# Eight more float32 tiles per layer cut into three float32r products, with their remainders made by transfers and GpSimd

## The chip, the cores and the metric

The kernel runs on one core of one Trainium2 chip. The metric is the device time of one execution in microseconds, taken as the median of several runs. A core has TensorE (PE: matmuls, and PEld: its weight loads), VectorE (DVE), ScalarE (ACT), GpSimd (POOL) and SyncE (SP), each with its own instruction queue that runs strictly in order, and 16 DMA engines that serve the transfers issued from SP's, ACT's and POOL's queues.

## The reference

Two layers over 272 tokens (16 meta tokens and 256 inputs) of width 1024. Each layer is a mixer (a gated causal depthwise convolution beside chunk-causal attention with low-rank projections, joined by two sets of gates), and a product-key expert layer that picks 16 experts per head and token out of 16384.

```python
h = _rmsnorm(x, mix_g); z = h @ w_in
conv_in, c_q, c_kv, k_rope, gate_logits = ...            # columns of z
u = conv_in[..., :512] * sigmoid(conv_in[..., 512:])
u = silu(_layernorm(_causal_depthwise_conv(u, conv_w, conv_b), ...))   # 31 taps
y_conv = u @ w_conv_out
...                                                      # q, k, v from c_q, c_kv, k_rope
y_mla = attention(q, k, v) @ w_mla_out
gates = sigmoid(gate_logits)                             # 2 x 1024 columns
x = x + (gates[..., :1024] * y_conv + gates[..., 1024:] * y_mla) @ w_out

hf = _rmsnorm(x, ffn_g)
q = (hf @ wq).reshape(T, 8, 2, 128)                      # 2048 columns
s = einsum('thpd,hpnd->thpn', q, keys)                   # 128 keys per half
sv, si = top_k(s, 16)                                    # then the top 16 of the 256 sums
a = einsum('ted,td->te', u_table[ids], hf)
x = x + einsum('te,ted->td', gelu(a) * w, v_table[ids])
```

## The kernel before, in words

Activations lie transposed: 128 of the 1024 features per partition block, the 272 tokens along the free dimension (256 in the second layer, where the meta tokens are no longer needed as outputs, `TQ`). Weights come in tiles of 128x1024, two to a transfer (a "pair", 1 MB), in the order in which TensorE uses them. SP issues the pairs; `dma_to` keeps a ring of four pair buffers (`wraw`) ahead, and a load waits until its buffer's last reader is done.

A tile of a projection is eight matmuls of 128x128 weights into one PSUM bank `z`. It is done in one of two ways. `ztile` multiplies in float32; the profile records each such matmul twice. `three` splits weights and activations into a part rounded to float32r ("high") and the remainder ("low") and adds three products, high by high, low by high and high by low, 24 matmuls. `high(i, n)` makes the rounded weight part on ACT, from the tile n places ahead; `low(i)` makes the remainder, in one of three ways: a subtraction on VectorE, the same on GpSimd, or (tiles 21, 23, 25, 27) a second copy on ACT with the sign turned followed by an accumulating transfer from POOL's queue that adds the raw weights. `kinds` says in which old buffers the two parts lie (`wq0`/`wq1`, `seln`/`upad`, `acc`/`sqa`, `kh`, `sq`).

Order of a layer: projections for attention; four pairs of convolution inputs (c = 0 to 3); sixteen gate tiles g0 to g15 (`TPG` names those cut in three); attention output, convolution output and merging tiles; sixteen query tiles (numbers 16 to 31 in `parts`, here query tiles 0 to 15); then the expert stages: 128 tiles of u weights (`A`) and 128 of v weights (`po`). Most token-expert pairs of 160 tokens go through dense matmuls in the expert stages, the other tokens through gathers: POOL fetches one 8 KB row per partition (`uv`), VectorE multiplies and adds it.

Beside the gate tiles, attention runs as a generator `att` stepped by hand twice a tile, and the 31 convolution taps run on VectorE (`conv`, `taps`, a number per tile in `TAPS`). For channel block 0 the first `KD` = 21 taps are products on ACT, added up by accumulating transfers into `part` (`conv2`); VectorE adds the three columns of `part` to `acc` at the end of `conv2`. When all taps are in, `layernorm` begins with the sum `tot` (tile name `zkr`), which a matmul with ones reads.

Beside the query tiles, VectorE picks top-16 values from the scores of the tile before (`scores`, `top16`), and a generator `early` prepares the expert numbers of the first tokens; `spread(0, 0, nc.sync)` sends them by a transfer on SP. Nine pairs of u weights are loaded ahead outside the ring: `EARLY` lists the pairs, `EPLACE` says after which query tile each is issued and into which buffer (own buffers `we`, or `kh`, `sq`, `g0`, `g1`, whose former contents are then done with; `g0` and `g1` hold the normalised input of the query tiles in two parts, `xq`).

Of the kernel before, what the change touches and what calls it, by code (L numbers as in the profile page):

```python
# [7 lines left out]
F32 = mybir.dt.float32  # L8
# [5 lines left out]
OP = mybir.AluOpType  # L14
# [8 lines left out]
KW = 31  # L23
# [2 lines left out]
WS = 16384.0  # L26
TAPS = [6, 6, 7, 8] + [9] * 12
KD = 21
TPG = (10, 11, 12, 13, 14, 15)
SCALE = 96 ** -0.5  # L30
NC_ = 58
GROUPS = ((64, 32), (64, 32))

EARLY = (0, 1, 2, 3, 8, 10, 12, 14, 16)
EPLACE = {1: (4, None), 4: (0, "kh"), 5: (5, None), 7: (6, None), 8: (7, None), 9: (1, "sq"), 11: (8, None), 12: (2, "g0"), 13: (3, "g1")}
JS = 63
MIXQ = {"xg", "uk", "qr", "rq_w", "rq_x", "rq_ym", "tkw0", "tkw1", "tkw2", "tkm", "sk", "scs", "qm",
        "wq0", "wq1", "seln", "upad", "acc", "sqa", "g0", "g1"}
LASTP = 2
RU = ((1.75, 1.45), (1.65, 1.33))  # L40
# [13 lines left out]
def trunk_kernel(ctx: ExitStack, tc: tile.TileContext, a: dict, out: bass.AP, dbg=None, stop=None):  # L54
    nc = tc.nc
# [9 lines left out]
    srcs = []  # L65
# [146 lines left out]
    for l in range(NL):  # L212
# [11 lines left out]
        def two(name):  # L224

            t_ = tw.tile([128, 8 * T], F32, name=name, tag=name)
            return t_[:, 0:2048]

        mixs = ExitStack()
        mixb = ExitStack()  # L230
        mpa = mixs.enter_context(tc.tile_pool(name=f"mixq{l}", bufs=1))
        mpb = mixb.enter_context(tc.tile_pool(name=f"mix{l}", bufs=1))

        class mp:

            @staticmethod
            def tile(shape, dt, name, **kw):
                return (tw if name in ("sq", "kh", "g0", "g1") else mpa if name in MIXQ else mpb).tile(shape, dt, name=name, **kw)
        zs = ExitStack()
        zp = zs.enter_context(tc.tile_pool(name=f"z{l}", bufs=1, space=PSUM))  # L240

# [423 lines left out]
        def conv2():  # L665

            for k in range(0, KD, 3):
                u_ = mp.tile([128, 3, T], F32, name="cp", bufs=2) if k else part
                for x in range(3):
                    S.activation(u_[:, x, t0:], upad[:, 0, k + x + t0:k + x + T], AF.Copy, scale=weight(0, k + x))  # L670
                    yield
                if k:
                    G.dma_start(part[:, :, t0:], u_[:, :, t0:], accum_op=OP.add)
            for _ in range(2):
                yield
            while ck[0] == KD:
                yield
            for x in range(3):
                V.tensor_add(acc[:, 0, t0:], acc[:, 0, t0:], part[:, x, t0:])
            yield  # L680

        parts = {}

        xhs_ = []
        kinds = {"g10": 0, "g11": 1, "g12": "k", "g13": 0, "g14": 1, "g15": "s", 0: "k", 1: 0, 2: 1, 3: "s", 4: "k",
                 19: "k", 20: "a", 21: "q", 22: "w", 23: "s", 24: "q", 25: "a", 26: "s", 27: "w"}

        def high(i, n):

            w_ = peek_w(n)  # L690
            x = kinds[i] if i in kinds else "aws"[(i - 5) % 3]
            if x == "w":
                hi, lo = [mp.tile([128, 1024], F32, name=f"wq{y}") for y in range(2)]
            elif x == "s":
                hi = mp.tile([128, 1024], F32, name="seln")
                lo = mp.tile([128, 1208], F32, name="upad")[:, 0:1024]
            elif x == "a":
                hi = mp.tile([128, 4 * T], F32, name="acc")[:, 0:1024]
                lo = mp.tile([128, 4 * T], F32, name="sqa")[:, 0:1024]
            elif x in (0, 1):  # L700
                if not xhs_:
                    xhs_.append(pp.tile([128, 8 * T], F32, name="xh"))
                hi = mp.tile([128, 1024], F32, name=f"wq{x}")
                lo = xhs_[0][:, 1024 * x:1024 * x + 1024]
            else:
                t_ = mp.tile([128, 8 * T], F32, name="kh" if x == "k" else "sq", tag="kh" if x == "k" else "sq")
                hi, lo = t_[:, 0:1024], t_[:, 1024:2048]
            parts[i] = hi.bitcast(F32R), lo.bitcast(F32R), w_
            S.activation(parts[i][0], w_, AF.Copy)
            if i in (21, 23, 25, 27):  # L710
                S.activation(parts[i][1], w_, AF.Copy, scale=-1.0)

        def low(i):

            hi, lo, w_ = parts[i]
            if i in (21, 23, 25, 27):
                G.dma_start(lo, w_, accum_op=OP.add)
            else:
                (G if i in (20, 22, 24, 26) else V).tensor_tensor(lo, w_, hi.bitcast(F32), op=OP.subtract)

        def three(i, p, xs, wc, cs, first, end, mid=None):

            hi, lo, _ = parts[i]
            for c in cs:
                s_ = slice((wc + c) * 128, (wc + c + 1) * 128)
                mm(p, hi[:, s_], xs[0][:, c, t0:], c == first, False)
                mm(p, lo[:, s_], xs[0][:, c, t0:], False, False)
                mm(p, hi[:, s_], xs[1][:, c, t0:], False, c == end)
                if c == 3 and mid:
                    next(mid, None)  # L730
# [78 lines left out]
        def taps(n, m, cs=(0, 1, 2, 3)):  # L809
            conv(n, cs)  # L810
            for _ in range(m):
                next(cvp, None)
# [4 lines left out]
        for c in range(4):  # L817
# [17 lines left out]
            if c == 2:  # L835
                xnh = big("uk", [8, T], F32R)
                xnl = mp.tile([128, 8, T], F32, name="un").bitcast(F32R)
                for k in range(8):
                    S.activation(xnh[:, k, t0:], xg[:, k, t0:], AF.Copy)
                    V.tensor_tensor(xnl[:, k, t0:], xg[:, k, t0:], xnh[:, k, t0:].bitcast(F32), op=OP.subtract)  # L840
            taps((0, 0, 8, 6)[c], (0, 3, 4, 4)[c], (1, 2, 3)[:max(c, 1)])
            next(att, None)

        gt = [big("g0", [8, T]), big("g1", [8, T])]
        ln = None
# [13 lines left out]
        for i in range(16):  # L859
# [3 lines left out]
                three(f"g{i}", z, (xnh, xnl), 0, range(8), 0, 7, ln if lnk == 2 else None)  # L863
            else:
                z = ztile(t0)
            new = [f"g{i + 2}"] if i + 2 in TPG else []
            ns = [1] if new else []
            for j in {13: (0,), 14: (1,)}.get(i, ()):
                new.append(j)
# [4 lines left out]
            S.activation(gt[i // 8][:, i % 8, t0:], z, AF.Sigmoid if ex else AF.Copy)  # L874
            if not ex:
                todo.append(i)
            if i >= 14:
                high(i - 12, 3)
            if i == 14:
# [100 lines left out]
        residual(7)  # L980
        normal(7)
        mixb.close()
        if stop == f"mix{l}":
            dump(stop, hT)
            for s_ in (asx, zs, mixs, twos, rp):
                s_.close()
            return
# [168 lines left out]
        for i in range(16):  # L1156
# [3 lines left out]
                three(16 + i, z, xq, 0, range(8), 0, 7)  # L1160
            else:
                z = ztile(t0)
            for k in {0: (2, 3), 1: (5,), 2: (4,), 3: (7,), 4: (6,), 5: (9,), 6: (8,), 7: (11,), 8: (10,)}.get(i, ()):
                high(16 + k, k - i - 1)
                low(16 + k)
            if i in EPLACE:
                k, n = early_[l][EPLACE[i][0]], EPLACE[i][1]
                raws[k] = (two(n).rearrange("p (a b) -> p a b", a=2) if n else
                           ep.tile([128, 2, 1024], F32, name=f"we{i}"))
                nc.sync.dma_start(raws[k], srcs[k])  # L1170
            qT_ = mp.tile([128, T], F32, name="qr", bufs=2)
            S.activation(qT_[:, t0:], z, AF.Copy)
            if not last:
# [576 lines left out]
```

## Time and profile before

| | us |
|---|---|
| median of 3 runs (1659.16 to 1660.91) | 1660.8 |
| the profiled execution | 1659.62 |
| its span | 1657.8 |
| TensorE busy | 1642.4 (99%) |
| VectorE busy | 1261.6 (76%) |
| ACT busy | 693.3 (42%) |
| POOL busy | 333.0 (20%) |
| DMA mean | 343 GB/s |

The page divides the span into 40 slices of about 41 us; a digit is the busy share of a slice in tenths. In a timeline a row is: start, duration, engine, line, operation, output and inputs by name, shapes, number of merged instructions, and in brackets the idle time before it and what ended it. A row of the chain of waits is start, duration, engine and what ran. The line L62 is the helper that issues every matmul, so matmuls are told apart by tile names. A windows row gives the stretch, its length, busy time and count of PE, PEld, DVE, ACT and POOL, then TensorE's granted clock, the DMA share and GB/s. TensorE's granted clock is full throughout.

### The profile page before, as it was taken

The page shows a single profiled execution, that of the slowest core. Times are in us where ns is not written, and L with a number is a line of the kernel's source. Part 1 is how long each engine was busy: PE and PEld are TensorE (multiplying, and loading weights), DVE is VectorE, ACT ScalarE, POOL GpSimd, SP SyncE. Part 2 cuts the span into 40 slices and gives each one's busy share as a digit, 9 for nine tenths or more (in the row PEclk, how much of TensorE's full clock was granted, in tenths as well). Part 3 has the DMA queues.
Part 4 walks back from the last instruction along what each step waited for, and adds up shares of the span by engine and source line. Part 5 has one row for each costly group of instructions (what it writes and reads, how often), then busy time and mean ns, then how long its engine had stood idle before and what let it go on. Part 6 is the DMA issues. An engine that isn't in the chain of part 4 may idle for free.

```text
span 1657.8 us, 30712 instructions
## 1 busy us (share of the span) xinstructions
PE 1642.4 (99%) x11827; PEld 1468.5 (89%) x11827; DVE 1261.6 (76%) x3082; ACT 693.3 (42%) x1803; POOL 333.0 (20%) x347
## 2 busy tenths in 40 slices
PE   9999999999999999999999999999999999999999
PEld 7679999999999999999986899999999997566655
DVE  5799899897898544444447998897877886788885
ACT  3565733435554111000024576433445443455554
POOL 0000033221222222222200100432211222233330
PEclk9999999999999999999999999999999999999999
DMA  6444697999999999999962746989999999999994
GB/s 249 113 128 177 242 345 298 424 383 424 416 423 418 424 424 423 424 424 424 417 259 85 176 153 242 340 348 396 362 425 409 409 391 411 420 425 425 424 425 191
DMA packets 86099, 568.52 MB, mean 343 GB/s; under 512 B 10328, under 2 KB 15384, under 8 KB 18744
## 3 DMA queue, kind: packets, MB, share of 16 engines
q1 hardware_dynamic: 50608, 338.51, 50.7%
q0 software_dynamic: 34560, 227.31, 35.0%
q8 instruction: 93, 1.52, 0.4%
q10 hardware_dynamic: 784, 0.74, 0.1%
q14 instruction: 54, 0.44, 0.1%
HBM read 556.18 MB, written 1.05 MB: 336 GB/s over the span
## 4 chain that ended last, share of the span: by engine, by line
PE 87%; DMA 8%; DVE 3%; ACT 1%; issue 1%; POOL 0%; SPq 0%; DVEq 0%; ACTq 0%; POOLq 0%
PE A L62 34%; PE po L62 25%; PE z L62 20%; DMA wraw<-vt 5%; PE aps L62 5%; PE wp L62 2%; DMA X<-vt 2%; DMA sqa<-wraw 1%; DVE acc L661 1%; PE xp L62 0%; PE sc L62 0%; DVE xh L1549 0%; PE wp L1262 0%; DVE tkw L1008 0%; ACT wr L1547 0%
## 5 line engine op out<-in xcount | busy, mean ns | idle before, releaser
L62 PE MATMUL A<-xh,wraw 128*128 128x160 f32 x3520 | 498.0, 300 | 0.0
L62 PEld LDWEIGHTS A<-xh,wraw 128*128 128x128 f32 x3520 | 481.1, 190 | 0.0
L62 PE MATMUL z<-xg,wraw 128*128 128x272 f32 (+2 forms) x832 | 194.1, 392 | 0.0
L1440 DVE SCALAR_TENSOR_TENSOR g<-g,xr 128x1024 f32<-128x1024 f32 x94 | 114.8, 1221 | 90.8 <-DMA g<-uv,iww 90.8
L62 PEld LDWEIGHTS z<-xg,wraw 128*128 128x128 f32 (+1 forms) x832 | 151.8, 189 | 35.0 <-issue 5.8
L1415 POOL DMA_INDIRECT g<-uv,iww x94 | 113.6, 1209 | 306.3 <-DVE va L1425 197.4
L1451 ACT ACTIVATE am<-am 128x1 f32<-128x1 f32 x208 | 40.9, 196 | 312.1 <-DVE g L1440 157.8
L62 PE MATMUL po<-Xh,wraw 128*128 128x160 f32 x1040 | 143.1, 300 | 1.0 <-DMA wraw<-vt 0.9
L62 PEld LDWEIGHTS po<-Xh,wraw 128*128 128x128 f32 x1040 | 141.5, 190 | 2.0 <-DMA wraw<-vt 2.0
L62 PE MATMUL po<-X,wraw 128*128 128x160 f32 x1008 | 138.4, 299 | 1.8 <-DMA wraw<-vt 1.3
L62 PEld LDWEIGHTS po<-X,wraw 128*128 128x128 f32 x1008 | 137.1, 190 | 2.7 <-DMA wraw<-vt 1.0
L1425 DVE SCALAR_TENSOR_TENSOR va<-g,am,va 128x1024 f32<-128x1024 f32 x91 | 116.5, 1281 | 0.3 <-ACT am L1452 0.2
L1340 ACT ACTIVATE ohA<-ohE,wlo 128x128 f16<-128x128 f16 x320 | 105.3, 428 | 5.2 <-DVE ohE L1337 4.4
L1440 DVE SCALAR_TENSOR_TENSOR kh<-kh,xr 128x1024 f32<-128x1024 f32 x48 | 58.6, 1221 | 42.5 <-DMA kh<-uv,iww 42.5
L1440 DVE SCALAR_TENSOR_TENSOR sq<-sq,xr 128x1024 f32<-128x1024 f32 x48 | 58.7, 1222 | 39.4 <-DMA sq<-uv,iww 39.4
L1415 POOL DMA_INDIRECT sq<-uv,iww x48 | 58.0, 1209 | 151.1 <-DVE va L1425 90.6
L1415 POOL DMA_INDIRECT kh<-uv,iww x48 | 59.9, 1248 | 140.4 <-DVE va L1425 92.8
L661 DVE SCALAR_TENSOR_TENSOR acc<-upad,cols,acc 128x272 f32<-128x272 f32 (+1 forms) x198 | 83.0, 485 | 0.2
L1351 ACT ACTIVATE Xh<-wp 128x260 f32<-128x260 f32 (+19 forms) x80 | 24.6, 307 | 131.5 <-DVE Xh L1348 124.8
L1425 DVE SCALAR_TENSOR_TENSOR va<-sq,am,va 128x1024 f32<-128x1024 f32 x48 | 61.5, 1281 | 5.5 <-ACT am L1452 5.5
L1425 DVE SCALAR_TENSOR_TENSOR va<-kh,am,va 128x1024 f32<-128x1024 f32 x48 | 61.5, 1282 | 3.7 <-ACT am L1452 3.7
L1452 ACT ACTIVATE am<-am,iww 128x1 f32<-128x1 f32 x208 | 61.3, 295 | 6.9
(503 smaller groups left out, 3075.0 us busy)
## 6 DMA issues: line engine op xcount, KB each, us to landing
wraw<-u SPq DMA_DIRECT2D x110, 1024.0 KB, 9.2
wraw<-vt SPq DMA_DIRECT2D x109, 1024.0 KB, 12.2
wraw<-w_in SPq DMA_DIRECT2D x27, 1024.0 KB, 4.7
X<-vt SPq DMA_DIRECT2D x17, 1024.0 KB, 11.4
wraw<-wq SPq DMA_DIRECT2D x16, 1024.0 KB, 4.8
we<-u SPq DMA_DIRECT2D x10, 1024.0 KB, 12.1
wraw<-w_out SPq DMA_DIRECT2D x8, 1024.0 KB, 4.6
wraw<-w_mla SPq DMA_DIRECT2D x4, 1024.0 KB, 5.1
```

What stands on the lines that cost most here:

```text
L62: PE.matmul(o, l, r, start=start, stop=stop, skip_group_check=True)
L661: V.scalar_tensor_tensor(acc[:, c, t0:], u_, weight(c, k), acc[:, c, t0:], op0=OP.mult, op1=OP.add)
L1340: S.activation(A_[1][:, t // 2, :, t % 2], E[0][:, t // 2, :, t % 2], AF.Copy, scale=wlo[:, 4 * b + t:4 * b + t + 1])
L1351: S.activation(x_, p[:, :, a:b].rearrange("p t j -> p j t"), AF.Copy, scale=1.0 / WS)
L1415: G.indirect_dma_start(out=g_, out_offset=None, in_=a[f"uv{l}"], in_offset=bass.IndirectOffsetOnAxis(ap=iww[i].bitcast(I32)[:, m // 16, 0, ...
L1425: V.scalar_tensor_tensor(vac[i], r, m_, vac[i], op0=OP.mult, op1=OP.add)
L1440: V.scalar_tensor_tensor(u_, u_, 1.0, xrs[i], op0=OP.mult, op1=OP.mult, accum_out=m_)
L1451: S.activation(m_, m_, AF.Gelu_apprx_tanh)
L1452: S.activation(m_, m_, AF.Copy, scale=iww[i][:, m // 16, 1, m % 16:m % 16 + 1])
```

## The change

Gate tiles 1, 3, 5 and 7 and query tiles 12 to 15 (28 to 31 in `parts`) become three-product tiles. The remainders of the gates and of tiles 30 and 31 are made by the accumulating transfer (now listed in `BYDMA`), those of 28 and 29 by subtraction on GpSimd. Tiles made by transfer run their products in another order: eight high by high, eight high by low activation part, and the eight with the remainder last. Gates 3 and 7 get a new buffer `gp`. In `conv2` the three adds of `part` wait until every tap of every block is in. The early pairs get new places; the ones in `sq`, `g0`, `g1` and one `we` come later, three `we` loads sooner, and since `g0` and `g1` are read until the last query tile, two loads are issued after tile 15. The work tiles of the top-16 (`ONLYQ`) go to a pool opened after the mixer's memory is released.

```diff
-TPG = (10, 11, 12, 13, 14, 15)
+TPG = (1, 3, 5, 7, 10, 11, 12, 13, 14, 15)
+ONLYQ = {"tkw0", "tkw1", "tkw2", "tkm", "scs", "qm"}
-EPLACE = {1: (4, None), 4: (0, "kh"), 5: (5, None), 7: (6, None), 8: (7, None), 9: (1, "sq"), 11: (8, None), 12: (2, "g0"), 13: (3, "g1")}
+EPLACE = {1: (4, None), 2: (5, None), 4: (0, "kh"), 5: (6, None), 6: (7, None), 13: (1, "sq"), 14: (8, None), 15: (2, "g0"), 15.5: (3, "g1")}
+BYDMA = ("g1", "g3", "g5", "g7", 21, 23, 25, 27, 30, 31)
-MIXQ = {"xg", "uk", "qr", "rq_w", "rq_x", "rq_ym", "tkw0", "tkw1", "tkw2", "tkm", "sk", "scs", "qm",
+MIXQ = {"xg", "uk", "qr", "rq_w", "rq_x", "rq_ym", "sk",
...
@@ conv2
-            for _ in range(2):
-                yield
-            while ck[0] == KD:
+            while min(ck.values()) < KW:
                 yield
             for x in range(3):
                 V.tensor_add(acc[:, 0, t0:], acc[:, 0, t0:], part[:, x, t0:])
-            yield
...
-        kinds = {"g10": 0, ..., 27: "w"}
+        kinds = {"g1": "v", "g3": "p", "g5": "v", "g7": "p", "g10": 0, ..., 27: "w", 28: "q", 29: "a", 30: "s", 31: "w"}
@@ high
-            if x == "w":
+            if x == "p":
+                t_ = mp.tile([128, 2048], F32, name="gp")
+                hi, lo = t_[:, 0:1024], t_[:, 1024:2048]
+            elif x in ("w", "v"):
                 hi, lo = [mp.tile([128, 1024], F32, name=f"wq{y}") for y in range(2)]
...
-            if i in (21, 23, 25, 27):
+            if i in BYDMA:
                 S.activation(parts[i][1], w_, AF.Copy, scale=-1.0)
@@ low
-            if i in (21, 23, 25, 27):
+            if i in BYDMA:
                 G.dma_start(lo, w_, accum_op=OP.add)
             else:
-                (G if i in (20, 22, 24, 26) else V).tensor_tensor(lo, w_, hi.bitcast(F32), op=OP.subtract)
+                (G if i in (20, 22, 24, 26, 28, 29) else V).tensor_tensor(lo, w_, hi.bitcast(F32), op=OP.subtract)
@@ three
+            if i in BYDMA:
+                for w_, x, f, e in ((hi, xs[0], first, None), (hi, xs[1], None, None), (lo, xs[0], None, end)):
+                    for c in cs:
+                        mm(p, w_[:, c * 128:(c + 1) * 128], x[:, c, t0:], c == f, c == e)
+                return
@@ convolution inputs, at the end of a pair
+            if c == 2:
+                high("g1", 3)
+                low("g1")
             taps((0, 0, 8, 6)[c], (0, 3, 4, 4)[c], (1, 2, 3)[:max(c, 1)])
             next(att, None)
+            if c == 3:
+                high("g3", 3)
+                low("g3")
@@ gate tiles
-            new = [f"g{i + 2}"] if i + 2 in TPG else []
+            new = [f"g{i + 2}"] if i >= 8 and i + 2 in TPG else []
...
+            if i in (1, 3):
+                high(f"g{i + 4}", 3)
+                low(f"g{i + 4}")
@@ after mixb.close()
+        qo.append(mixs.enter_context(tc.tile_pool(name=f"qo{l}", bufs=1)))
@@ query tiles
-            for k in {0: (2, 3), 1: (5,), ..., 8: (10,)}.get(i, ()):
+            for k in {0: (2, 3), 1: (5,), ..., 8: (10,), 9: (12,), 10: (13,), 11: (14, 15)}.get(i, ()):
                 high(16 + k, k - i - 1)
                 low(16 + k)
-            if i in EPLACE:
-                k, n = early_[l][EPLACE[i][0]], EPLACE[i][1]
...
+            for e in (i, i + 0.5):
+                if e in EPLACE:
+                    k, n = early_[l][EPLACE[e][0]], EPLACE[e][1]
...
```

More of the change, by code (lines that the diff above doesn't have):

```diff
@@ L230, in trunk_kernel @@
         mixb = ExitStack()
+        qo = []
         mpa = mixs.enter_context(tc.tile_pool(name=f"mixq{l}", bufs=1))
@@ L237, in tile @@
             def tile(shape, dt, name, **kw):
-                return (tw if name in ("sq", "kh", "g0", "g1") else mpa if name in MIXQ else mpb).tile(shape, dt, name=name, **kw)
+                return (tw if name in ("sq", "kh", "g0", "g1") else qo[0] if name in ONLYQ else mpa if name in MIXQ else mpb).tile(shape, dt, name=name, **kw)
         zs = ExitStack()
@@ L679, in conv2 @@
                 V.tensor_add(acc[:, 0, t0:], acc[:, 0, t0:], part[:, x, t0:])
-            yield
         parts = {}
         xhs_ = []
-        kinds = {"g10": 0, "g11": 1, "g12": "k", "g13": 0, "g14": 1, "g15": "s", 0: "k", 1: 0, 2: 1, 3: "s", 4: "k",
-                 19: "k", 20: "a", 21: "q", 22: "w", 23: "s", 24: "q", 25: "a", 26: "s", 27: "w"}
+        kinds = {"g1": "v", "g3": "p", "g5": "v", "g7": "p", "g10": 0, "g11": 1, "g12": "k", "g13": 0, "g14": 1, "g15": "s", 0: "k", 1: 0, 2: 1, 3: "s", 4: "k",
+                 19: "k", 20: "a", 21: "q", 22: "w", 23: "s", 24: "q", 25: "a", 26: "s", 27: "w", 28: "q", 29: "a", 30: "s", 31: "w"}
         def high(i, n):
@@ L1162, in trunk_kernel @@
                 z = ztile(t0)
-            for k in {0: (2, 3), 1: (5,), 2: (4,), 3: (7,), 4: (6,), 5: (9,), 6: (8,), 7: (11,), 8: (10,)}.get(i, ()):
+            for k in {0: (2, 3), 1: (5,), 2: (4,), 3: (7,), 4: (6,), 5: (9,), 6: (8,), 7: (11,), 8: (10,), 9: (12,),
+                      10: (13,), 11: (14, 15)}.get(i, ()):
                 high(16 + k, k - i - 1)
                 low(16 + k)
-            if i in EPLACE:
-                k, n = early_[l][EPLACE[i][0]], EPLACE[i][1]
-                raws[k] = (two(n).rearrange("p (a b) -> p a b", a=2) if n else
-                           ep.tile([128, 2, 1024], F32, name=f"we{i}"))
-                nc.sync.dma_start(raws[k], srcs[k])
+            for e in (i, i + 0.5):
+                if e in EPLACE:
+                    k, n = early_[l][EPLACE[e][0]], EPLACE[e][1]
+                    raws[k] = (two(n).rearrange("p (a b) -> p a b", a=2) if n else
+                               ep.tile([128, 2, 1024], F32, name=f"we{i}"))
+                    nc.sync.dma_start(raws[k], srcs[k])
             qT_ = mp.tile([128, T], F32, name="qr", bufs=2)
```

## The prediction

> **What bounds the kernel now.** I read the page first: busy times, slices, chain. Its lines carry the first answer.
>
> ```profile
> span 1657.8 us, 30712 instructions
> PE 1642.4 (99%) x11827; PEld 1468.5 (89%) x11827; DVE 1261.6 (76%) x3082; ACT 693.3 (42%) x1803; POOL 333.0 (20%) x347
> GB/s 249 113 128 177 242 345 298 424 383 424 416 423 418 424 424 423 424 424 424 417 259 85 176 153 242 340 348 396 362 425 409 409 391 411 420 425 425 424 425 191
> PE 87%; DMA 8%; DVE 3%; ACT 1%; issue 1%; POOL 0%; SPq 0%; DVEq 0%; ACTq 0%; POOLq 0%
> ```
>
> TensorE (PE) is busy 99% of the span and holds 87% of the chain, so matmul time removed counts wherever no other engine catches up. The bytes per slice show two regimes in each layer: the mixer and query projection (slices 1 to 6 and 21 to 27 of 40) run at 85 to 350 GB/s, while the expert stages after them sit near 424. The change edits only the first regime, so I next read those stretches, in time order: the chain, then VectorE's (DVE) timeline with its waits, then ACT, POOL and SP.
>
> **The matmul saving.** Rows of the chain: plain tiles (eight float32 products, 16 records) and tiles cut in three products (24 records), 272 columns in layer 1 and 256 in layer 2.
>
> ```profile
> 63.53 7.34 PE z L62 x32
> 171.20 27.13 PE z L62 x216
> 921.52 6.91 PE z L62 x32
> 1005.40 25.53 PE z L62 x216
> ```
>
> A plain tile is 7.34/2 = 3.67 us, a three-product tile 27.13/9 = 3.01: 0.66 saved. In layer 2 it is 6.91/2 - 25.53/9 = 3.46 - 2.84 = 0.62. Each layer converts eight tiles (gates 1, 3, 5, 7; query tiles 12 to 15): 8 x 0.66 + 8 x 0.62 = 10.2 us of TensorE time gone.
>
> **The gate half: does VectorE let it through?** VectorE runs the convolution taps there almost without a break. These are its waits, the end of its convolution sum, and the TensorE product that reads it; layer 1, then layer 2.
>
> ```profile
> 80.34 1.48 DVE L469 TENSOR_TENSOR kh<-kh,aps 96x272 f32<-96x272 f32 x4 [0.58 <-PE aps L62]
> 112.43 1.36 DVE L492 TENSOR_REDUCE mx<-aps 128x1 f32<-128x144 f32 x4 [1.55 <-PE aps L62]
> 132.60 0.92 DVE L747 TENSOR_TENSOR zkr<-zkr,acc 128x272 f32<-128x272 f32 x2
> 133.87 0.73 PE L62 MATMUL aps<-zkr,ones 128*128 128x272 f32 x2
> 938.58 1.36 DVE L492 TENSOR_REDUCE mx<-aps 128x1 f32<-128x144 f32 x4 [0.94 <-PE aps L62]
> 949.57 1.36 DVE L492 TENSOR_REDUCE mx<-aps 128x1 f32<-128x144 f32 x4 [1.98 <-PE aps L62]
> 970.19 0.67 PE L62 MATMUL aps<-zkr,ones 128*128 128x256 f32 x2 [0.67 <-DVE zkr L747]
> ```
>
> Nothing leaves VectorE: the new gate tiles' remainders are made by accumulating transfers, and the three adds of the transferred taps move to the end of the taps, 3 x 0.46 (the zkr row's 0.92/2) on both sides of the move: nothing, as VectorE is busy from one place to the other. What VectorE can gain is its waits on TensorE. Layer 1: 0.58 + 1.55 = 2.13, while TensorE gains 4 x 0.66 = 2.64. The sum was ready at 133.52 and used at 133.87, so the new wait is (133.52 - 2.13) - (133.87 - 2.64) = 0.16 us. Layer 2: waits of 0.94 + 1.98 = 2.92 exceed TensorE's 4 x 0.62 = 2.48, so that half passes whole and the 0.67 wait stays.
>
> Their price on ACT and POOL: each of the four tiles adds two copies on ACT and one transfer on POOL's queue.
>
> ```profile
> 1045.36 1.05 ACT L711 ACTIVATE sqa<-wraw 128x1024 fp32r<-128x1024 f32 x1
> 63.67 2.67 ACT L839 ACTIVATE uk<-xg 128x272 fp32r<-128x272 f32 x8
> 94.77 0.47 ACT L498 ACTIVATE pr<-aps,nb,sc 128x144 f32<-128x144 f32 x1 [3.97 <-DVE nb L493]
> 75.72 3.93 PE L62 MATMUL z<-xg,wraw 128*128 128x272 f32 x16
> DMA to landing us min/median/max: 4.1/4.9/8.3
> ```
>
> Two copies are 2.1 us. For gate 7 they fall into the 3.97 us that ACT waits before the second softmax; cover gone, they would delay it by up to 2.1. Gate 1 is the tight one: ACT is free of the operand copies at 66.3, the pair is done at 68.4, and transfers of this queue at this place (the taps' own, last line) land in 4.1 to 8.3, so by 72.5 to 76.7. Gate 1 begins at 75.72 and reads the remainder only after 16 of its 24 products, 2.0 us later. I take zero; if it took 12.6 us (the longest below) it would cost 3.3 per layer.
>
> **The query half: when do the remainders arrive?** In order: the scattered-index copy that holds ACT, POOL's subtraction and its four scalings, the landing times of today's four such transfers per layer, tile 14's start in both layers, and a stall of today's tile 9.
>
> ```profile
> 230.96 1.91 ACT L1064 ACTIVATE tx<-it 128x2048 f16<-128x2048 f16 x1 [3.71 <-DVE it L1062]
> 224.77 2.39 POOL L719 TENSOR_TENSOR upad<-wraw,seln 128x1024 fp32r<-128x1024 f32 x1 [0.39 <-ACT seln L709]
> 227.12 2.95 POOL L1205 TENSOR_TENSOR xh<-xg,rq_ym 128x272 f32<-128x272 f32 x4
> DMA to landing us min/median/max: 6.2/9.1/12.6
> 246.94 3.83 PE L62 MATMUL z<-xg,wraw 128*128 128x272 f32 x16
> 1060.59 1.91 ACT L1064 ACTIVATE tx<-it 128x2048 f16<-128x2048 f16 x1 [2.99 <-DVE it L1062]
> 1077.17 3.62 PE L62 MATMUL z<-xg,wraw 128*128 128x256 f32 x16
> 1059.56 0.38 PE L62 MATMUL z<-g,sqa 128*128 128x256 f32 x1 [1.67 <-DMA sqa<-wraw]
> ```
>
> Tiles 12 and 13 are subtracted on GpSimd, 14 and 15 by transfer, and all four go through POOL in order, between scalings of 2.95/4 = 0.74. Layer 1: ACT is free at 232.9, tile 12's copy ends 233.9, its subtraction 236.3, a scaling 237.1, tile 13's subtraction 239.5, a scaling 240.2; then tile 14's transfer starts. TensorE reaches tile 14 at 246.94 - 2 x 0.66 = 245.6 and needs the remainder 16 x 0.126 = 2.0 later, 247.6. At the median 9.1 it lands at 249.3: a wait of 1.7. Layer 2: 1062.5, 1063.6, 1065.9, 1066.7, 1069.1, 1069.8; needed at 1077.17 - 1.67 - 2 x 0.62 + 1.9 = 1076.2, landing 1078.9: a wait of 2.7. So 4.4 us are given back; tile 15's transfer, one issue later, is needed 3 us later still and is covered. Ends: at 6.2 nothing, at 12.6 it is 5.2 + 6.2 = 11.4. I take the median because it is the same instruction in the same stage, and a pair of early loads joins the queue right at that time. [...]
>
> The reordering of the products (all those with the high part first) also applies to today's transferred tiles. Tile 9 of layer 2 stalls 1.67 for a remainder it now needs 1.9 later: 1.7 gained (0 if its transfer lands that much later).
>
> **Early pairs, queues, memory.** Pairs 2 and 3 of the expert weights are loaded after tile 15, since their buffers now hold the query operand until then. On SP they stand behind the index spread, which waits for VectorE.
>
> ```profile
> 255.31 0.62 SPq L1150 DMA_DIRECT2D iww<-ew  x1
> 254.72 1.42 PE L62 MATMUL sc<-uk,qr 128*128 128x128 f32 x8
> 257.09 4.61 PE L62 MATMUL A<-xh,kh 128*128 128x160 f32 x32 [0.59 <-ACT idxT L1036]
> 266.76 8.45 PE L62 MATMUL A<-xh,g 128*128 128x160 f32 x61
> 255.00:265.00 10.00, 9.30 (x73) 8.73 (x73) 9.39 (x72) 4.75 (x10) 3.55 (x4) 1.00 0.28 88
> wraw<-w_out SPq DMA_DIRECT2D x8, 1024.0 KB, 4.6
> kh<-uv,iww POOLq DMA_INDIRECT x1, 14.5
> 260.54 1.08 POOL L1415 DMA_INDIRECT X<-uv,iww  x1 [30.46 <-DVE ts L1006]
> ```
>
> They issue at about 255.9. The expert stage will start 2.37 after tile 15 ends, at 254.72 - 4 x 0.66 + 1.7 + 2.37 = 256.2, and reads pair 2 after 266.76 - 257.09 = 9.7, at 265.8: 9.9 us of cover. The window shows DMA at 88 GB/s there, and a quiet megabyte takes 4.6, so I take zero. The worst near row is a gather in the crowd, 14.5: 4.6 per layer. Pair 1 (after tile 12, issue near 241) has 19 us. Behind the two loads on SP wait only the meta-row copies of layer 1, which need VectorE later still.
>
> The top-16 work tiles move to a pool of their own, outside the memory that the first gathers fill; those gathers waited for VectorE's top-16 until 260.54 though the index was sent at 255.31. They may start up to 2.5 us sooner per layer; I take nothing, since the expert weights, not they, are next on TensorE.
>
> **What the expert stages do with an earlier start.** DMA is full there, so an earlier TensorE could just wait for weights.
>
> ```profile
> PE po L62 <- DMA wraw<-vt: 2.2, 6, 0.7
> 836.05 1.28 DVE L1425 SCALAR_TENSOR_TENSOR va<-g,am,va 128x1024 f32<-128x1024 f32 x1
> 842.91 1.85 PE L62 MATMUL xp<-zs,va 128*128 128x16 f32 x16
> ```
>
> Waits for weights are 2.2 us in all, and layer 1's last gather is added 5.6 us before TensorE needs it (842.91 - 837.33). TensorE will be 2.5 + 2.6 - 1.7 = 3.4 early, VectorE and so the gathers at least 2.1: a lag of 1.3, inside that 5.6. I take zero.
>
> **Sum.** -10.2 + 0.16 - 1.7 + 4.4 = -7.3 us. The profiled execution took 1659.62, 1.2 under the median 1660.8 of the runs; 1652.3 in its terms is 1653.5 against the median. No change means within 0.2%, 3.3 us.
>
> **Rivals.** (1) The remainders land in time (6.2): -11.7, 1649.1. For it: by the new places three loads leave the time just before it. Against: by SP's order three megabyte loads (pair 1, a ring pair, pair 16) go out near 241, and the 9.1 median. [...] (2) The transfer-full expert stages give the query half back and only the gates' shift survives, 2.1 + 2.5 = 4.6: 1656.2. For it: 424 GB/s in nearly every slice; against: 2.2 us of waits and 5.6 of cover. Chance 0.17. (3) The remainders land at worst (12.6): -0.3, 1660.5, chance 0.09. (4) Slower: pair 2 is late. Its place is the third pair of each expert stage; the loads share DMA with the first gathers. At 14.5 us it costs 2 x 4.6 = 9.2, giving 1662.7 with the rest as summed; it turns the sign above 9.9 + 3.7 = 13.6 us. Against: DMA is nearly idle when they issue. Chance 0.08.
>
> **Numbers.** My forecast 0.46 (its own range 1651 to 1656), the rivals as given. Faster by over 0.2%: 0.46 + 0.20 + most of 0.17, 0.81; same 0.09 and the remainder, 0.12; slower 0.07. The range runs from rival 1 with gathers a little early, 1647, to between rivals 2 and 3, 1658.
>
> **What would show it.** Gates 1, 3, 5, 7 at 3.0 and 2.84 us; waits at 112 and 949 gone from VectorE; a wait of TensorE on the transfers into upad (tile 14) of 1 to 3 us in each layer, and none on sqa; the third expert pair without a wait; the last gather add of layer 1 still ahead of its sum. I am wrong if TensorE waits on the loads into g0 and g1, on gate 1's remainder, or if waits on wraw<-vt grow by more than 2 us.

## The result, and the profile after

The change made the kernel slower: 1672.8 us (median of 6 runs, 1668.5 to 1675.3) against 1659.2 for the kernel before on the same chip (6 runs, 1657.0 to 1660.9). The ratio is 1.0078, 95% interval 1.0061 to 1.0095. The profiled execution took 1673.24 us, its span is 1671.5, so 13.7 more than the span of before. The prediction was 1653.5, its range 1647 to 1658.

The page, the parts that were shown of before:

```profile
span 1671.5 us, 31046 instructions
PE 1643.3 (98%) x11955; PEld 1474.8 (88%) x11955; DVE 1261.4 (75%) x3082; ACT 717.8 (43%) x1831; POOL 356.9 (21%) x363
PE 79%; DMA 11%; DVE 5%; ACT 2%; issue 1%; POOL 1%; SPq 0%; DVEq 0%; POOLq 0%; ACTq 0%
```

TensorE's busy time did not fall by 10 us, it rose by 0.9, and of the 8 points of share that TensorE lost in the chain of what ended last DMA and VectorE (DVE) took 5. Fewer products and slower products cancel in the busy time: the mean granted clock of this execution is 0.993, of before 1.000, and 0.007 of the span is 11.7 us (an estimate; it counts waits at the lower clock too). The rest of the loss is waits. TensorE's waits (us in all, times, longest), and the rows of the chain that belong to transfers (start, duration, both in us):

```profile
PE z L64 <- DMA wq<-wraw: 7.0, 2, 4.1
PE z L64 <- DMA gp<-wraw: 2.6, 1, 2.6
PE aps L64 <- DVE zkr L755: 2.1, 2, 1.6
```

```profile
69.51 8.83 DMA part<-cp
240.26 13.37 DMA wq<-wraw
913.67 11.48 DMA part<-cp
931.72 10.74 DMA part<-cp
1079.56 13.50 DMA wq<-wraw
```

Two places, each once per layer. `wq<-wraw` at 240 and 1079 is tile 15's remainder: 13.4 and 13.5 us from issue to landing. `part<-cp` is a transfer of taps; their landing times were 4.1/4.9/8.3 before and are now:

```profile
DMA to landing us min/median/max: 4.4/8.1/11.5
```

To put the loss on places, I cut the span at six points of TensorE's timeline: a product of z near 59 us, the product of zkr (end of the gate half), the first expert pair (end of the query half), and in layer 2 its first product, zkr and the first expert pair. Four of these rows in after:

```profile
133.56 0.70 PE L64 MATMUL aps<-zkr,ones 128*128 128x272 f32 x2 [0.50 <-DVE zkr L755]
257.89 6.53 PE L64 MATMUL A<-xh,kh 128*128 128x160 f32 x32 [0.59 <-ACT idxT L1054]
978.46 1.03 PE L64 MATMUL aps<-zkr,ones 128*128 128x256 f32 x2 [1.60 <-DVE zkr L755]
1097.46 6.58 PE L64 MATMUL A<-xh,kh 128*128 128x160 f32 x32 [0.53 <-ACT idxT L1054]
```

Before, the same stages took 74.6, 123.2 and 590.9 us (gates, queries, experts of layer 1), then 122.2, 116.3 and 571.3. The table gives each kernel's difference from these in us, worked out from the start times in its own trace; a minus is time saved. The times are medians of 5 to 12 runs, the ratios are to the runs of the kernel before on the same chip, with their 95% intervals. The stages come from one profiled execution each; single executions of a kernel scatter by 2 to 9 us. Furthest from their medians are those of gates_only (3.7 above), gates_notrans (1.9 below) and queries_warm (2.1 below).

```
kernel            us      ratio [95%]             gates1 query1 expert1 gates2 query2 expert2
after           1672.8  1.0078 [1.0061, 1.0095]    0.0   +1.1   +3.2   +4.2   +2.7   +2.7
gates_only      1666.1  1.0037 [1.0023, 1.0051]   +0.2   -0.1   +0.5   +9.6   -0.6   +0.5
gates_pool      1666.3  1.0038 [1.0025, 1.0051]   +3.0   -0.1   +0.9   +3.3   +0.6   -0.1
gates_notrans   1657.2  0.9986 [0.9977, 0.9995]   -0.8   -0.1   -0.1   -1.1   -2.0    0.0
gates_57        1659.4  0.9988 [0.9977, 0.9999]   -1.3   -0.1   +0.2   +2.1   -0.5   -0.6
queries_only    1667.2  1.0039 [1.0026, 1.0052]   +0.5   +1.3   +1.3   +0.9   +1.8   +1.4
queries_pool    1660.9  1.0004 [0.9995, 1.0013]   +0.5   -1.9   +3.2   +0.9   -1.6   +1.7
queries_notrans 1655.9  0.9976 [0.9967, 0.9986]   +0.5   -2.7   +0.6   +1.0   -3.1   -0.1
queries_quiet   1671.6  1.0069 [1.0055, 1.0083]   +0.5   -2.0   +6.4   +0.9   +0.6   +6.7
queries_warm    1663.1  1.0017 [1.0009, 1.0026]   +0.5   +0.3   +0.4   +0.9   +0.1   -0.5
neither         1661.5  1.0005 [0.9996, 1.0014]   +0.5   -0.1   +1.8   +0.9   -0.5   +0.4
q1214           1654.8  0.9966 [0.9953, 0.9979]    0.0   -2.0   +0.1    0.0   -3.7   +1.1
best            1658.2  0.9987 [0.9978, 0.9996]   -1.3   -1.4   +0.8   +2.2   -1.1   +0.5
```

**The gate half.** GpSimd's queue (POOL), ACT and VectorE in time order; the first row is of before, the same transfer as in the second:

```profile
72.82 0.89 POOL L673 DMA_DIRECT2D part<-cp  x1 [3.83 <-ACT cp L670]
78.87 0.85 POOL L676 DMA_DIRECT2D part<-cp  x1 [8.39 <-DMA part<-cp]
925.70 1.29 POOL L676 DMA_DIRECT2D part<-cp  x1 [10.60 <-DMA part<-cp]
```

```profile
78.42 0.93 ACT L673 ACTIVATE cp<-upad,cols 128x272 f32<-128x272 f32 x2 [6.19 <-DMA part<-cp]
79.26 1.04 ACT L712 ACTIVATE gp<-wraw 128x1024 fp32r<-128x1024 f32 x1
925.24 0.91 ACT L673 ACTIVATE cp<-upad,cols 128x256 f32<-128x256 f32 x2 [8.71 <-DMA part<-cp]
```

```profile
88.26 0.18 DVE L507 RECIPROCAL sm<-sm 128x4 f32<-128x4 f32 x1 [2.34 <-ACT pr L501]
934.74 0.18 DVE L507 RECIPROCAL sm<-sm 128x4 f32<-128x4 f32 x1 [4.97 <-ACT pr L501]
945.05 0.18 DVE L507 RECIPROCAL sm<-sm 128x4 f32<-128x4 f32 x1 [2.49 <-ACT pr L501]
```

The taps' transfers all add into one tile (`part`), so GpSimd issues each only when the last has landed. Gate 1's 512 KB go out just before the first of them; that one lands late, and GpSimd stands 8.4 us (10.6 in layer 2) before it can issue the next, in layer 1 6 us later than before (78.87, before 72.82). The taps' two buffers (`cp`) stay full, and ACT, which works in order, stands 6.2 us (8.7 in layer 2) before its next copy into one. Behind that copy stand gate 3's copies and the softmax, and VectorE waits for the softmax: 2.3 us in layer 1, 7.5 in layer 2. Gate 3's remainder is late by the same chain in layer 2, the 2.6 us on gp.

**The query half.** TensorE at tile 15, and its granted clock (the last three columns of a window are clock, DMA share and GB/s):

```profile
253.67 1.27 PE L64 MATMUL z<-g,wq 128*128 128x272 f32 x8 [2.83 <-DMA wq<-wraw]
1093.10 2.08 PE L64 MATMUL z<-g,wq 128*128 128x256 f32 x8 [4.12 <-DMA wq<-wraw]
```

```profile
250.00:260.00 10.00, 6.58 (x39) 5.53 (x38) 9.16 (x48) 1.65 (x7) 1.27 (x2) 0.75 0.79 279
1090.00:1100.00 10.00, 6.37 (x25) 6.07 (x26) 6.81 (x35) 1.75 (x6) 1.88 (x2) 0.56 0.86 317
```

TensorE stands 2.8 and 4.1 us with the high part's 16 products done. After that its clock is 0.75 and 0.56 of full in the ten microseconds around (in windows of two microseconds it reads 0.50 from 1092 to 1100 us and 1.00 again from 1102), and the first expert pair, the same 32 products as before, takes 6.53 and 6.58 us instead of 4.61: 1.9 us more in each layer, which appear in the table under "expert". No wait on tile 14 (upad) is left, none on sqa, and none on pairs 2 and 3.

### The profile page after: what moved, and what is told of

It is laid out like the page before. It is cut to its first block, busy times and chain, and to the rows that moved or that the text cites. A ratio compares the mean times of both kernels' runs of the same rounds, so it can differ in the third digit from the quotient of the medians.

```text
span 1671.5 us, 31046 instructions
## 1 busy us (share of the span) xinstructions
PE 1643.3 (98%) x11955; PEld 1474.8 (88%) x11955; DVE 1261.4 (75%) x3082; ACT 717.8 (43%) x1831; POOL 356.9 (21%) x363
## 4 chain that ended last, share of the span: by engine, by line
PE 79%; DMA 11%; DVE 5%; ACT 2%; issue 1%; POOL 1%; SPq 0%; DVEq 0%; POOLq 0%; ACTq 0%
PE A L64 34%; PE po L64 26%; PE z L64 12%; DMA wraw<-vt 5%; PE aps L64 3%; DVE acc L664 3%; PE wp L64 2%; DMA part<-cp 2%; DMA wq<-wraw 2%; DMA X<-vt 1%; DMA wraw<-wq 1%; PE xp L64 0%; PE sc L64 0%; DVE mx L495 0%; DMA wraw<-w_in 0%
## 5 line engine op out<-in xcount | busy, mean ns | idle before, releaser
L1435 POOL DMA_INDIRECT g<-uv,iww x94 | 117.4, 1249 | 308.5 <-DVE va L1445 195.6
L64 PE MATMUL z<-xg,wraw 128*128 128x272 f32 (+2 forms) x576 | 134.4, 394 | 0.4 <-DMA wraw<-w_in 0.4
L64 PEld LDWEIGHTS z<-xg,wraw 128*128 128x128 f32 (+1 forms) x576 | 104.3, 188 | 27.4 <-issue 4.9
```

What stands on the lines that cost most here:

```text
L64: PE.matmul(o, l, r, start=start, stop=stop, skip_group_check=True)
L1435: G.indirect_dma_start(out=g_, out_offset=None, in_=a[f"uv{l}"], in_offset=bass.IndirectOffsetOnAxis(ap=iww[i].bitcast(I32)[:, m // 16, 0, ...
```

## Experiments

**One half at a time.** The query half's edits undone (tiles 12 to 15 in float32, early pairs as before), then the gate half's undone:

```diff
# gates_only, and EPLACE as before
-            for k in {..., 8: (10,), 9: (12,),
-                      10: (13,), 11: (14, 15)}.get(i, ()):
+            for k in {..., 8: (10,)}.get(i, ()):
...
# queries_only, and no high and low of these gates
-TPG = (1, 3, 5, 7, 10, 11, 12, 13, 14, 15)
+TPG = (10, 11, 12, 13, 14, 15)
...
```

> The change with its query half taken back (query tiles 12 to 15 plain, early pairs at their old places); gate tiles 1, 3, 5, 7, the late adds, the product order and the moved work tiles stay. Theory A (transfers crowd each other on POOL's queue: a remainder's transfer holds up the taps' transfers, ACT waits for the two product buffers, the softmax and with it VectorE come late): the loss of the changed kernel's gates stays, layer 1 about even (-0.3 us at the first expert projection) and layer 2 late by about 5.8 us, less 1.7 for the stall on sqa that goes: about 1663 us. Rival B (the gates do gain, and the loss is all in the query half): about 1653.

> The change with its gate half taken back. Theory A: tile 15's remainder lands 13 us after issue as in the changed kernel, TensorE waits 3 to 4 us in each layer and runs the first expert pair at a lower clock: about +3 us a layer and 1 to 2 later, so 1666 us. Rival B (tile 15 is late only because the gates' transfers and stalls came before): no wait on wq, about 1652.

Each half alone loses, as theory A of each had it: 1666.1 and 1667.2 against 1659.5 for before. The two losses, 6.6 and 7.7, add up to about the change's 13.6. The gate half loses in layer 2's gates (+9.6; with the same gate edits the change lost 4.2 there, so the price of the late chain varies from execution to execution), the query half at its own place and in what follows.

**The remainders by GpSimd instead of a transfer**, first the gates', then tiles 14 and 15:

```diff
# gates_pool; in queries_pool 30 and 31 are moved in the same way
-BYDMA = ("g1", "g3", "g5", "g7", 21, 23, 25, 27, 30, 31)
+BYDMA = (21, 23, 25, 27)
...
-                (G if i in (20, 22, 24, 26, 28, 29) else V).tensor_tensor(lo, w_, hi.bitcast(F32), op=OP.subtract)
+                (G if i in ("g1", "g3", "g5", "g7", 20, 22, 24, 26, 28, 29) else V).tensor_tensor(lo, w_, hi.bitcast(F32), op=OP.subtract)
...
```

The second copy on ACT goes with the transfer; the order of the products stays.

> As gates_only, but the remainders of gate tiles 1, 3, 5, 7 are subtracted on GpSimd (one ACT copy each and no transfer), products in the same order. Theory A: nothing holds up the taps' transfers, the gate half gains its 4 x 0.66 + 4 x 0.62 = 5.1 and 1.7 on sqa less some tenths: about 1653. Rival C (ACT's copies are too many: half of them stay): half of the loss stays, about 1659. Rival D (GpSimd's reads hold up VectorE's two-input taps): VectorE's taps grow and the sum zkr is later than in gates_only: 1662 or more.

> As queries_only, but the remainders of tiles 14 and 15 too are subtracted on GpSimd. Theory A: they end near 242 and 244.5 us in layer 1, before tiles 14 and 15 ask for them; no wait, full clock, 8 x 0.64 = 5.1 and 1.7 on sqa gained: about 1653. Rival E (TensorE now outruns the gathers and the early pairs 2 and 3, which come after tile 15): TensorE waits at the third expert pair or the waits on wraw<-vt grow, and the time stays near 1659.

Neither came near 1653. VectorE's taps grew beside GpSimd's subtractions, as rival D of gates_pool had it; that it is GpSimd's reads is not shown. In the gates, layer 1 (59 to 137 us; busy time, mean ns), VectorE's taps in gates_pool, then in before:

```profile
L665 DVE SCALAR_TENSOR_TENSOR acc<-upad,cols,acc 128x272 f32<-128x272 f32 x99 | 45.2, 521 | 0.1
L663 DVE TENSOR_SCALAR acc<-upad,cols 128x272 f32<-128x272 f32 x4 | 3.6, 918 | 0.0
```

```profile
L661 DVE SCALAR_TENSOR_TENSOR acc<-upad,cols,acc 128x272 f32<-128x272 f32 x99 | 42.3, 493 | 0.1
```

2.9 us on the first group, and 2.0 on the second (1.6 in all before): 4.9 us in a stage whose whole gain was to be 2.6. In queries_pool two rows show it without arithmetic, GpSimd's subtraction and a VectorE instruction of 64 columns beside it; behind them the same instruction in queries_notrans, where GpSimd is idle:

```profile
242.88 2.40 POOL L723 TENSOR_TENSOR wq<-wraw,wq 128x1024 fp32r<-128x1024 f32 x1
242.94 2.39 DVE L1100 TENSOR_SCALAR q<-po 128x64 int32<-128x64 int32 x1
259.08 0.62 SPq L1160 DMA_DIRECT2D iww<-ew  x1
```

```profile
242.56 0.20 DVE L1102 TENSOR_SCALAR q<-po 128x64 int32<-128x64 int32 x1
```

VectorE's instruction took as long as GpSimd's and ended with it (245.33 and 245.28 us). The next top-16 ran 3.8 us later than in before (248.10 instead of 244.33), and the index spread went out at 259.08 instead of 255.31 (255.88 in queries_notrans). The expert stage of layer 1 then gave the saving back (+3.2). That the late index is the reason is not shown: the waits that TensorE's rows show in that stage are 3.9 us, before 2.7, which is 1.2 of the 3.2, and rival E's wait on pairs 2 and 3 is in no row.

**The transfers alone taken away.** All instructions of ACT, TensorE and VectorE stay:

```diff
-                S.activation(parts[i][1], w_, AF.Copy, scale=-1.0)
+                S.activation(parts[i][1], w_, AF.Copy, scale=0.0 if i in NOTR else -1.0)
...
+            if i in NOTR:
+                return
```

> As gates_only, but the remainders of gates 1, 3, 5 and 7 are written as zeros by ACT's second copy and not transferred: the correction by the weights' remainder is left out for these four tiles, all instructions of ACT, VectorE and TensorE stay. Theory A (the 512 KB transfers stand in GpSimd's queue before those of the taps, the taps' buffers come free late, ACT waits for them in order and the softmax behind it): ACT waits on the taps' transfers no more than before, the waits of VectorE for the softmax go, zkr starts near 132.4 us in layer 1 (133.87 less 2.1, plus 0.6 for the late adds) and about 1.5 us earlier than before in layer 2, time 1654 to 1657. Rival (ACT is late because of its eight extra copies, 1.05 us each, or the late adds): ACT's waits shrink but zkr stays where gates_only has it, time 1662 to 1666.

> As queries_only, but the remainders of query tiles 14 and 15 are zeros written by ACT and not transferred: the correction by the weights' remainder is left out for these two tiles. This is the query half with its transfers' lateness taken away and GpSimd left as it is. Theory A (tile 15's late transfer, the wait and the slower clock after it are all of the loss): no wait before tile 15, first expert pair at 4.61 us and starting near 255.1 in layer 1 (257.09 less 2.64, plus 0.6), time 1653 to 1655. Rival (the expert stages are full of transfers and give an earlier start back): the first pair starts near 255.1 as well, but layer 2 starts no earlier than 847.5 to 848.0 and the time is 1657 to 1660, like the kernel with GpSimd remainders.

Both first theories held in what they said of the cause. Without its transfers the gate half goes from 1666.1 to 1657.2 us, the query half from 1667.2 to 1655.9: the transfers cost 9.0 and 11.3 (8.5 and 10.5 by the ratios, each give or take 3). Against what both have in common, the next experiment's 1661.5, the tiles saved 4.3 and 5.6 (3.2 and 4.8 by the ratios), where the prediction's sum had 5.0 and 5.1. So the saving was there, and the lateness of the transfers cost about twice as much. The gates still did not give all: VectorE waits for the softmax once in each layer, and the taps' transfers are late there without the gates' (in layer 2 the first takes about 9.6 us). ACT has eight more copies, which I take for the reason; that is not shown.

```profile
87.44 0.18 DVE L508 RECIPROCAL sm<-sm 128x4 f32<-128x4 f32 x1 [1.58 <-ACT pr L502]
927.04 0.18 DVE L508 RECIPROCAL sm<-sm 128x4 f32<-128x4 f32 x1 [2.58 <-ACT pr L502]
```

The query half kept most of its lead through layer 1: -2.7 at its end, and +0.6 in the expert stage behind it.

**Neither half**: what is left is the order of the products, the late adds and the top-16 pool.

> No new tile is cut in three products; what stays of the change is the order of the products of the four transferred tiles of before, the three adds of the transferred taps behind all others, and the top-16 work tiles in a pool of their own. Theory A (the late adds are not free: they were the cover of ACT's copy for the next weight cut, VectorE waits 0.58 us on it in layer 1 and about 0.75 in layer 2; the new order takes away the stall of 1.67 on sqa): the product of zkr starts about 0.6 us later in layer 1 and 1.0 later in layer 2 (counted from that layer's start), TensorE does not wait on sqa, and the two cancel: 1659.3 us (1658 to 1660.5). Theory B (the adds cost nothing, as the prediction had it): zkr as before, 1657.8.

1661.5, 1.0005 [0.9996, 1.0014]: no change that can be measured, as theory A had it, though its 1659.3 was 2 us too low. The late adds cost what it said: 0.5 us in layer 1 and 0.9 in layer 2. VectorE waits for ACT's copy where before it was adding:

```profile
123.18 1.23 DVE L722 TENSOR_TENSOR xh<-wraw,wq 128x1024 fp32r<-128x1024 f32 x1 [0.58 <-ACT wq L712]
962.49 1.23 DVE L722 TENSOR_TENSOR xh<-wraw,wq 128x1024 fp32r<-128x1024 f32 x1 [0.74 <-ACT wq L712]
```

The wait on sqa is gone, yet layer 2's query stage gained only 0.5. Slow products took most of the rest: TensorE's wait for zkr is now 1.6 us (0.7 before), and behind it, from 970 to 980 us, the clock reads 0.83, where it reads 1.00 in before. queries_only and queries_warm, the same program between zkr and tile 15, price this: both wait 1.6 us for zkr, the clock falls to 0.83 only in the first, and from zkr to the start of query tile 11 it takes 95.26 us, the second 93.84. That is 1.4 us.

Its expert stage of layer 1 is 1.8 us longer. A single wait of 1.87 us for an expert weight at 740 us makes all its waits for weights only 0.6 longer than before; the larger part is the clock, 0.83 from 740 to 750. Other kernels with the same order do not have this wait; I take it as scatter of that transfer-full stage, not as an effect of the change.

**Is it the loads beside tile 15's transfer?** Pairs 1 and 16 moved behind tile 15:

```diff
-6: (7, None), 13: (1, "sq"), 14: (8, None), 15: (2, "g0"), 15.5: (3, "g1")}
+6: (7, None), 15: (1, "sq"), 15.25: (8, None), 15.5: (2, "g0"), 15.75: (3, "g1")}
...
```

> As queries_only, but the loads of early pair 1 (into sq) and of the sixteenth early pair, issued with tiles 13 and 14, now follow tile 15, behind them pairs 2 and 3: one megabyte is left (the ring's) where three went out right behind tile 15's transfer. Theory A (tile 15's transfer is late because those loads share the DMA engines with it): it lands in 7 to 10 us instead of 13.4, the wait before tile 15 is under 1 us instead of 2.7 and 3.5, the first expert pair is back near 4.6 us; a load moved late can cost some of it, time 1658 to 1663. Rival (two transfers of that kind on one queue run one after the other, whatever SP loads): it still lands in 12 us or more, the waits stay within 0.7 us of those of queries_only and the time is 1665 to 1668.

```profile
248.21 1.27 PE L64 MATMUL z<-g,upad 128*128 128x272 f32 x8 [0.44 <-DMA upad<-wraw]
261.59 0.67 PE L64 MATMUL A<-xh,sq 128*128 128x160 f32 x3 [1.83 <-DMA sq<-u]
1086.17 1.21 PE L64 MATMUL z<-g,upad 128*128 128x256 f32 x8 [3.38 <-DMA upad<-wraw]
1105.80 6.41 PE L64 MATMUL A<-xh,g 128*128 128x160 f32 x23 [3.54 <-DMA g<-u]
```

Neither theory whole. With one load left beside them, TensorE does not wait for tile 15's remainder, but now tile 14's is the late one: issued at 1076.06, it lands about 1086.1, ten microseconds. Tile 15's landing is in no row; it was there when TensorE read it, about 13 us after its issue. So moving two of the three loads did not make the pair of transfers quick. The megabyte that is left went out 0.6 us ahead of them, and no run has the pair without any load, so what the loads add stays open. And the loads moved late were missed: 1.8 and 3.0 us (sq, g) in layer 1, 3.5 in layer 2, the mechanism of rival 4, with a clock of 0.76 behind the last (1100 to 1110 us). It is slower than queries_only.

**Is it the idling that slows TensorE's clock?** Products of the high part repeated into an unused bank while TensorE waits:

```diff
+                    if i == 31 and w_ is lo:
+                        zd = sp.tile([128, 512], F32, name="zd")[:, :TQ]
+                        nf = (21, 28)[l]
+                        for c in range(nf):
+                            mm(zd, hi[:, c % 8 * 128:(c % 8 + 1) * 128], x[:, c % 8, t0:], c == 0, c == nf - 1)
```

> As queries_only, with 21 (layer 1) and 28 (layer 2) further products of tile 15's high part into a bank that nobody reads, placed where TensorE waits 2.7 and 3.5 us for tile 15's remainder: TensorE works through the wait. Theory A (TensorE's clock falls because it idles there): the remainder's eight products take 1.0 us instead of 1.57 and 2.07, the first expert pair starts about 1.3 us earlier in each layer, 1664.5 us (1663 to 1666). Rival (the clock falls for another reason, or only the wait costs): the eight products stay slow or the first pair does not come earlier, 1666.5 to 1668.5.

Tile 15's last products and the next group in queries_warm, then in queries_only:

```profile
1085.13 1.21 PE L64 MATMUL z<-g,wq 128*128 128x256 f32 x8 [1.06 <-DMA wq<-wraw]
1086.18 1.41 PE L64 MATMUL sc<-uk,qr 128*128 128x128 f32 x8
```

```profile
1088.36 2.07 PE L64 MATMUL z<-g,wq 128*128 128x256 f32 x8 [3.54 <-DMA wq<-wraw]
1090.23 1.66 PE L64 MATMUL sc<-uk,qr 128*128 128x128 f32 x8
```

Behind these two waits it is. With useless work in the wait the eight products take 1.21 instead of 2.07, the time from them to the first expert pair falls from 4.06 to 2.99 us in layer 2 and from 4.52 to 3.48 in layer 1, and the kernel from 1667.2 to 1663.1. Of these 4.1 us the products behind the waits explain at most 2.1: in layer 2 the remainder was 0.8 us later than in queries_only, counted from the start of tile 15. Another 1.4 of layer 2's query stage are luck, the clock that did not fall behind zkr, long before the useless products. The rest lies in expert stages that also came out shorter.

**What is free of harm.** gates_57 converts gates 5 and 7 alone, best adds query tiles 12 and 13, q1214 takes query tiles 12 to 14 and no gate; all three have the adds at their old place.

```diff
# q1214
...
-                      10: (13,), 11: (14, 15)}.get(i, ()):
+                      10: (13, 14)}.get(i, ()):
...
-6: (7, None), 13: (1, "sq"), 14: (8, None), 15: (2, "g0"), 15.5: (3, "g1")}
+6: (7, None), 12: (1, "sq"), 14: (2, "g0"), 14.5: (3, "g1"), 15: (8, None)}
```

> Of the gate half only gates 5 and 7 are cut in three products, by transfers; the adds of the taps at their old place. Theory A (gates 1 and 3 did the harm: their transfers stand where the taps' first three are issued 5 us apart, while gates 5 and 7 fall where the taps' come 10 us apart): ACT waits less than 1 us on the taps' buffers, VectorE has no wait on the softmax beyond those of before, zkr comes about 1.2 us earlier in each layer, 1656 to 1658.5. Rival (any such transfer delays the taps' chain): VectorE waits on pr or on part, 1660 or more.

> What the runs so far say is free of harm: gates 5 and 7 by transfers, query tiles 12 and 13 by GpSimd, tiles 14 and 15 in float32, the adds of the taps at their old place, pairs 2 and 3 after tile 13. Theory A: 2 x 0.66 + 2 x 0.62 saved in each half, 5.1 us, and 0.5 from the order of the products in layer 2; the expert stage of layer 1 keeps about 1 of it: 1655 (1653.5 to 1656.5). Rival (GpSimd's subtractions hold VectorE's top-16 up, and the index spread comes late): the spread is issued after 257 us, first expert pair not before 256.5, 1658 or more.

> Query tiles 12 and 13 by GpSimd and tile 14 by a transfer that is alone (tile 15 stays in float32), issued one tile earlier than in the change; the adds of the taps at their old place; pairs 2 and 3 after tile 14, the sixteenth pair after tile 15. Theory A (tile 15's 13.4 us came from two such transfers and three loads at once): tile 14's lands within 8 us and TensorE waits less than 0.5 us for it; saved are 3 x 0.66 and 3 x 0.62, so 1655.5 to 1657. Rival (a transfer there is slow whatever else runs): TensorE waits 2 us or more on upad in layer 2, 1659 or more.

gates_57 came to 1659.4, outside theory A's range. It did what was expected in layer 1 (-1.3) and what its rival said in layer 2 (+2.1), where the taps' transfers are late again and the adds at their old place now wait for the last of them:

```profile
941.45 0.51 ACT L673 ACTIVATE cp<-upad,cols 128x256 f32<-128x256 f32 x1 [5.22 <-DMA part<-cp]
955.68 1.34 DVE L682 TENSOR_TENSOR acc<-acc,part 128x256 f32<-128x256 f32 x3 [2.53 <-DMA part<-cp]
```

best inherits that and comes to 1658.2, 0.9987 [0.9978, 0.9996], against an expected 1655. q1214 beats both kernels: 1654.8, 0.9966 [0.9953, 0.9979]. One transfer alone, issued a tile earlier, is in time; no wait on it is left in either layer, the query stages are 2.0 and 3.7 us shorter, and layer 1's expert stage keeps all of it (+0.1). q1214 changes three things about that transfer at once: it is alone, it goes out a tile earlier, and the loads beside it are placed otherwise. Which of them makes it timely is not separated.

## Why the prediction was wrong

Seven statements can be judged, in the order of the sum.

- **10.2 us of TensorE time saved: right.** q1214's three tiles gave 2.0 us in layer 1, 0.68 each against the predicted 0.66; with the transfers gone the two halves gave 4.3 and 5.6 by the medians, 9.9 together (8.0 by the ratios).
- **"Nothing leaves VectorE", gate half through it: the step that failed first.** The sum priced the two copies and the landing of gate 1, which it had in time, and it was: TensorE did not wait for it. The sum did not ask what is queued behind gate 1's transfer. The row for that was on the table (the taps' own transfers, 4.1/4.9/8.3 us, two buffers, issued 5 us apart): with transfers of 512 KB ahead of them the chain is late, ACT waits in order for a buffer, and the softmax behind it is late. The gate stage, where the sum had -2.5 in each layer, came out at 0.0 in layer 1 and +4.2 in layer 2. The sum's bound of 3.3 per layer was a bound on gate 1's own wait, not on this.
- **The moved adds cost nothing: wrong by 1.4 us.** They are the same work on both sides of the move, but they had covered ACT's copy for the next cut. Covers have to be looked up on both sides of a move.
- **4.4 us back for tile 14's late remainder, "tile 15's transfer, one issue later, ... is covered": the second step that failed.** Tile 14's landed in time; tile 15's took 13.4 and 13.5 us, beyond the longest of before (12.6), and TensorE waited 2.8 and 4.1. I took the second of two transfers on one queue to land as soon after its issue as the first. The wait itself, 7.0 us, was within 2.6 of the predicted 4.4; the larger part of the miss stands in the next point.
- **A clock at full speed throughout: not stated as a step, and wrong.** Each wait was followed by slow products, worth 1.9 us at the first expert pair of each layer in the change, on top of the wait. No term of the sum carried it, as no wait of before (the longest 2.0 us) was followed by it. Waits of 1.6 us at zkr and 1.87 at 740 were, in neither.
- **1.7 us from the order of the products: right in q1214** (query stage of layer 2 -3.7, of which three tiles make 1.9 and the order the rest); in neither, where zkr comes late, only 0.5 of it is left, and the slow products behind that wait, 1.4 us, are about what is missing.
- **Pairs 2 and 3 covered, expert stages take nothing: right** for the change as made; no wait on g0 or g1, and q1214 kept its lead through layer 1. queries_quiet shows where that cover ends.

Put together for the change's own trace, the six stages are 13.9 us over before (the start is 0.3 earlier). Of these 3.8 are the slow first expert pairs, 8.0 lie in the gate and query stages, which were to give 7.3 back, and 2.1 are left in the two expert stages. Part of the 8.0 is the clock too: it reads 0.83 from 930 to 940 us, behind the wait on gp, and 0.93 and 0.90 from 970 to 990, behind the wait for zkr, an estimated 3.4 us in all (0.17, 0.07 and 0.10 of ten microseconds each). The 2.1 no experiment explains; the lone wait in neither shows that such amounts come and go there.

None of the four rivals came true (the first had a chance of 0.20). The one on the slower side, pair 2 late, put the danger on SP's loads, and it lay on GpSimd's queue; that the change gains less than it saves because a queue is late was in rival 3, with the worst landing of before (12.6) as its bound, and the landings went beyond it.

That the gates' four transfers together delay the taps' is shown: gates_notrans takes away nothing else. For gate 1's alone the rows of layer 1 speak, where the first taps' transfer has only gate 1's ahead of it: 8.83 us, and 5.16 in gates_notrans. In layer 2 it took 11.48, but about 9.6 in gates_notrans too, so there something else has the larger part. What stays open is whether the transfers delay the taps' by their place in the queue or by sharing the DMA engines; no run has the two on separate queues.

## What to carry to other kernels

Before a transfer is put on a queue, list what is behind it there and how many buffers stand between it and an engine that works in order; here the late buffers held ACT up for 6.2 and 8.7 us, and the softmax behind paid for it (2.3 and 7.5 us of VectorE's waits), while TensorE did not wait for gate 1's remainder. Price two transfers issued together by the time that both need (here the second landed after 13.4 and 13.5 us), and give a TensorE wait a second price, for the slow products after it (waits of 1.6 us were enough here, though not each time). Three tiles per layer with one transfer, a tile earlier, gained 5.4 us where eight with six transfers lost 13.6.

## What the runs showed of the hardware

- A VectorE instruction of 0.20 us took 2.39 beside a GpSimd subtraction of 2.40 that had started 0.06 us earlier (queries_pool), and the two ended 0.05 us apart. Not every instruction grows so: two MAX8 beside the subtraction before it, at 241.47 us, took 0.47 us, and at 249.89, with none beside them, 0.47 as well.
- TensorE's clock after a wait does not follow the length of the wait alone. After 2.83 us the ten-microsecond window reads 0.75, after 4.12 it reads 0.56 (0.50 in after from 1092 to 1100 us), after 1.6 at zkr in neither 0.83. But after the same 1.6 in queries_warm most single products behind it take 0.28 us, where in queries_only they take 0.41, and after 3.38 in queries_quiet the clock reads 1.00:

```profile
1085.00:1090.00 5.00, 3.83 (x32) 3.83 (x33) 4.79 (x19) 0.83 (x3) 0.00 (x0) 1.00 0.14 28
```

What else decides is not shown.
- Of two 512 KB transfers that add into SBUF, issued 0.6 us apart, the second landed 13.4 and 13.5 us after its issue (after). In after a taps' transfer 0.5 to 1.2 us behind one of 512 KB took 8.7 to 11.5 us, and one that went out 11.8 us behind such a transfer (at 951.41) took 9.9; in before, with none ahead, the taps' took 4.1 to 8.3. Distance alone does not make one quick: those of before, about 6 us or more apart, took 6.2 to 12.6. q1214's, issued at 1066.21, was there when TensorE read it without a wait 7.5 us later.
